# Whole-row transfers around the SSD, early splits of reloaded inputs, and unread products in the conformer's LayerNorm

## The chip, the cores and the metric

The kernel runs on one core of a Trainium2 chip. The metric is the device time of one execution in microseconds (us), as the median of several runs.

## The reference

One inference step of a two-layer decoder trunk, in float32, for a prompt of 512 tokens and a sample group of 8 sequences of 8 tokens. The 576 tokens share all weights; the model has 1024 channels.

```python
# layer 0
xn = rms_norm(x); proj = xn @ w_in_ab           # z | x,B,C | dt | u
ya = mamba2(proj[z, xBC, dt])                   # causal conv of 4, silu, SSD, gate, group norm
yb = s5(proj[u])                                # complex diagonal SSM, gelu, then
yb = y * sigmoid(y @ w_glu + b_glu)             # the gated linear unit (GLU)
x  = x + concat(ya, yb) @ w_out_ab
x  = x + square(relu(rms_norm(x) @ w_ff1)) @ w_ff2
# layer 1
h  = xn @ w_pw1 + b_pw1; h = h[:C] * sigmoid(h[C:])
h  = causal_depthwise_conv(h, 31 taps)
h  = silu(layer_norm(h, ln_w, ln_b))            # mean and variance over 1024 channels
x  = x + h @ w_pw2 + b_pw2
x  = x + square(relu(rms_norm(x) @ w_ff1)) @ w_ff2
y  = rms_norm(x)
```

In the SSD, heads go in 4 groups of 4, and the prompt in 4 chunks of 128 tokens; the 64 sample tokens make a fifth chunk. Each chunk needs exp(cum[i] - cum[j]) for its heads, where cum is the running sum of the log decays.

## The kernel before, in words

**Products.** Activations lie with channels on the 128 partitions and 576 tokens in the free dimension. Each float32 operand is split in two (`split`, L266; `split_scaled`, L257): ScalarE (ACT) writes the high part, VectorE (DVE) the rest. `mm` (L228) multiplies a 128 x 1024 weight tile with eight activation tiles: hi*hi, hi*lo and lo*hi, in two halves of 288 tokens, 48 matmuls on TensorE (PE) for one output tile. `load` (L217) brings the weight tile in on SP's DMA queue and splits it on ACT and DVE (L224, L225), with a priority offset of 3000.

**Order.** The kernel is written once in program order, and a scheduler lays the instructions on each engine's queue by priority and by its own simulated time. `high_priority(n)` moves a block n places up in that order. The queues are fixed then: on the chip each engine, and SP's queue of DMAs, takes its instructions strictly in turn, so one that waits holds all behind it. Tiles of a tag share a ring of buffers: the 17 of tag "B" hold split activations, the 3 of tag "t" hold what comes out of a product or is loaded for one step.

**Layer 0** (`mixer0`, L1061). The products of `w_in` come first: eight for the S5, one for dt, then 24 for the SSD, in four groups of six (B, C, two of x, two of z). Each of the 24 results is copied out of PSUM by `stash` (L759) and stored to DRAM. `side` runs after each product and puts in the other work: first the S5's outputs (`s5_y`, stored to `yg`), then one causal convolution (`a_conv`, L767) and one step of each running SSD group (`a_group`, L879), with an offset of 54 (HPS). Then `reload` (L1154) loads the eight tiles of `yg` and splits them for the eight GLU products; after these it reloads `ybd` for the products with the second half of `w_out`, and last `yad` (the first SSD group's output) for the first half. There the tiles of the other groups are used first, the reloaded ones last.

**The convolution.** `a_conv` loads one stashed tile into `xb`, the prompt and the sample by two DMAs (L773, L774), since each sample sequence gets three tokens of history in front of it: 8 pieces of 11 columns, of which 8 (32 bytes) come from DRAM. DVE scales in place (L776, L777), ACT makes the first tap into `o` (L782), DVE adds three taps (L784) and, after a tanh, closes the silu with one instruction over 600 columns (L787). Two DMAs (L788, L789) store prompt and sample to `xsd`. `xb` and `o` share a ring of three buffers. `a_group` loads its inputs from `xsd` (L889), transposes them on PE (L899), and per chunk loads cum of its 4 heads on all partitions (L943: 4 pieces of 512 bytes each) and exp(cum) (L957); old states come from the input (L924), and the sample's part of the output uses them (L928).

**The conformer** (`conformer`, L1204). The channel means are sums on PE (`mean`, L1301) over the eight convolved tiles; the tile of block 7 is finished last, by DVE (L1389, L1391). Then DVE subtracts the mean (L1259), ACT squares (L1261), DVE adds squares in pairs (L1253), and PE sums each pair over channels by matmuls of one column (`tsum`, L1256). DVE takes the reciprocal root, PE spreads it over the partitions (L323), and DVE and ACT normalise, apply silu and split (L1272 to L1277) in front of the eight products of `w_pw2`.

## Time and profile before

| what | value |
| --- | --- |
| median of 3 runs | 1638.1 us (1636.99 to 1638.96) |
| the profiled execution | 1634.01 us; span 1632.2 us |
| PE busy | 1574.1 us (96% of the span) |
| DVE busy | 1056.4 us (65%) |
| ACT busy | 642.3 us (39%) |
| DMA read, written | 184.1 MB, 34.2 MB |
| mean granted PE clock | 0.975 of full speed |

The profiled execution is 4.1 us under the median of the runs. The span goes from the first to the last instruction; 1.8 us of the execution's time lie around it. A granted clock of 1.0 is 2.4 GHz and 0.5 is 1.2 GHz; it has these two levels, and a number between is a mean over a stretch.

### The profile page before, as it was taken

What the parts mean: (1) busy time and instruction counts of PE and PEld (TensorE: products, weight loads), DVE (VectorE), ACT (ScalarE), POOL (GpSimd) and SP (SyncE); (2) the same over time, 40 slices, a digit from 0 to 9 for tenths busy, and PEclk for the clock granted to TensorE, in tenths of its full rate; (3) what the DMA queues carried; (4) which work ended last, traced back from release to release, by engine and by line L of the source; (5) the groups of instructions that cost most, each with busy time, mean ns of one, the idle gap of its engine ahead of it and who ended that gap; (6) DMA issues with size and microseconds to landing.
All of it is one profiled execution on the core that took longest, in us unless ns stands there. A gap on an engine that the chain in (4) does not pass through costs nothing.

```text
span 1632.2 us, 28709 instructions
## 1 busy us (share of the span) xinstructions
PE 1574.1 (96%) x11765; PEld 1549.3 (95%) x11765; DVE 1056.4 (65%) x1757; ACT 642.3 (39%) x1084; POOL 4.3 (0%) x42
## 2 busy tenths in 40 slices
PE   7999998989899999999999999997899999999997
PEld 6999998889899999999999999996899999999996
DVE  7968986688865547677744457997554444434466
ACT  4243377775643343332222243332443322222243
POOL 0000000000000000000000000000000000000000
PEclk9999999979899999999999999998899999999998
DMA  5644587988863234454322235541122222222233
GB/s 189 184 120 142 158 226 220 298 251 241 241 229 136 78 96 160 156 135 105 101 79 78 91 133 154 167 136 45 42 88 79 78 91 78 79 90 78 91 118 135
DMA packets 185907, 220.18 MB, mean 135 GB/s; under 512 B 92560, under 2 KB 128400, under 8 KB 185776
## 3 DMA queue, kind: packets, MB, share of 16 engines
q1 hardware_dynamic: 182112, 217.03, 44.3%
q8 instruction: 92, 1.51, 0.4%
q10 hardware_dynamic: 3664, 1.32, 0.3%
q14 instruction: 39, 0.32, 0.1%
HBM read 184.10 MB, written 34.20 MB: 134 GB/s over the span
## 4 chain that ended last, share of the span: by engine, by line
PE 84%; DVE 8%; DMA 5%; issue 1%; ACT 1%; SPq 0%; ACTq 0%; DVEq 0%
PE mm L239 76%; PE pc L1326 2%; DVE acc L1389 1%; DVE lo L225 1%; PE yoff L928 1%; DMA by<-s5bc 1%; PE bc L323 1%; DMA eb<-ecd 1%; DMA xsd<-cvo 1%; PE s5s L613 1%; PE kt L572 1%; PE tsum L293 1%; DVE u L589 1%; PE mu L1301 0%; PE yps L952 0%
## 5 line engine op out<-in xcount | busy, mean ns | idle before, releaser
L224 ACT ACTIVATE hi<-raw 128x1024 fp32r<-128x1024 f32 x217 | 229.7, 1059 | 729.4 <-PE mm L239 633.3
L239 PE MATMUL mm<-fxh,hi 128*128 128x288 f32 x1920 | 417.6, 299 | 14.6 <-ACT hi L224 10.4
L225 DVE TENSOR_TENSOR lo<-raw,hi 128x1024 fp32r<-128x1024 f32 x217 | 264.8, 1221 | 248.0 <-ACT hi L224 243.4
L239 PE MATMUL mm<-fxh,lo 128*128 128x288 f32 x1920 | 415.4, 298 | 0.1
L239 PE MATMUL mm<-fxl,hi 128*128 128x288 f32 x1920 | 414.9, 297 | 0.0
L239 PEld LDWEIGHTS mm<-fxh,hi 128*128 128x128 f32 x1920 | 311.5, 190 | 16.3 <-ACT hi L224 11.3
L239 PEld LDWEIGHTS mm<-fxh,lo 128*128 128x128 f32 x1920 | 311.0, 190 | 1.0 <-DVE lo L225 0.7
L239 PEld LDWEIGHTS mm<-fxl,hi 128*128 128x128 f32 x1920 | 311.1, 190 | 0.5 <-issue 0.2
L239 PE MATMUL mm<-gh,lo 128*128 128x288 f32 x1024 | 229.1, 295 | 1.1 <-DVE lo L225 1.1
L239 PE MATMUL mm<-gh,hi 128*128 128x288 f32 x1024 | 229.6, 295 | 0.0
L239 PE MATMUL mm<-gl,hi 128*128 128x288 f32 x1024 | 229.2, 295 | 0.0
L239 PEld LDWEIGHTS mm<-gh,lo 128*128 128x128 f32 x1024 | 167.9, 188 | 1.5 <-DVE lo L225 1.5
L239 PEld LDWEIGHTS mm<-gl,hi 128*128 128x128 f32 x1024 | 168.3, 188 | 0.0
L239 PEld LDWEIGHTS mm<-gh,hi 128*128 128x128 f32 x1024 | 167.9, 188 | 0.0
L363 DVE TENSOR_TENSOR fft<-mm,r2B 128x576 f32<-128x576 f32 x56 | 42.3, 756 | 116.3 <-PE mm L239 116.3
L1389 DVE SCALAR_TENSOR_TENSOR acc<-hb,vec,acc 128x512 f32<-128x512 f32 x110 | 82.2, 747 | 1.5
L357 DVE TENSOR_TENSOR gl<-ffr,gh 128x576 fp32r<-128x576 f32 x64 | 48.4, 757 | 1.9
L356 DVE TENSOR_TENSOR ffr<-ffr 128x576 f32<-128x576 f32 x64 | 48.5, 757 | 1.6
L355 ACT ACTIVATE gh<-ffr 128x576 fp32r<-128x576 f32 x64 | 43.9, 686 | 2.1
L364 DVE TENSOR_TENSOR x<-x,fft 128x576 f32<-128x576 f32 x56 | 42.3, 756 | 1.6
L784 DVE SCALAR_TENSOR_TENSOR cvo<-xb,vh,cvo 128x600 f32<-128x600 f32 x48 | 40.2, 838 | 1.0 <-ACT cvo L782 0.5
L353 ACT ACTIVATE ffr<-mm 128x576 f32<-128x576 f32 x64 | 40.5, 633 | 0.0
(340 smaller groups left out, 1890.0 us busy)
## 6 DMA issues: line engine op xcount, KB each, us to landing
raw<-w_ff SPq DMA_DIRECT2D x136, 512.0 KB, 3.5
raw<-w_in SPq DMA_DIRECT2D x33, 512.0 KB, 3.8
raw<-w_pw SPq DMA_DIRECT2D x24, 512.0 KB, 3.6
dm<-dwm SPq DMA_DIRECT2D x16, 576.0 KB, 5.6
h<-ass SPq DMA_DIRECT2D x16, 512.0 KB, 4.9
raw<-w_out SPq DMA_DIRECT2D x16, 512.0 KB, 3.6
U<-ud SPq DMA_DIRECT2D x16, 288.0 KB, 4.0
prd<-pj SPq DMA_DIRECT2D x16, 288.0 KB, 2.4
```

What stands on the lines that cost most here:

```text
L224: self.last = [nc.sync.dma_start(raw, src), nc.scalar.activation(hi, raw, AF.Copy), eng.tensor_tensor(lo, raw, hi.bitcast(F32), op=ALU.sub ...
L225: eng.tensor_tensor(lo, raw, hi.bitcast(F32), op=ALU.subtract)]
L239: nc.tensor.matmul(ps[:, h, :H], w[:, k], a[:, h * H:(h + 1) * H], start=n == 0, stop=n == 23)
L353: nc.scalar.activation(h2(r), ps, AF.Relu)
L355: nc.scalar.activation(hi, r, AF.Square)
L356: nc.vector.tensor_tensor(r, r, r, op=ALU.mult)
L357: nc.vector.tensor_tensor(lo, r, hi.bitcast(F32), op=ALU.subtract)
L363: nc.vector.tensor_tensor(h2(t), ps, rB, op=ALU.mult)
L364: nc.vector.tensor_tensor(x[m], x[m], t, op=ALU.add)
L784: nc.vector.scalar_tensor_tensor(o[:, 0:600], xb[:, k:k + 600], self.half("acw", 16 * k + m), o[:, 0:600], op0=ALU.mult, op1=ALU.add)
L1326: nc.tensor.matmul(pc[:, g * 128:g * 128 + 128], w[:, j * 128:j * 128 + 128], hq[:, g, j:j + 128], start=j == 0, stop=j == 8)
L1389: nc.vector.scalar_tensor_tensor(ap, hb[:, k:k + NP], w(k), ap, op0=ALU.mult, op1=ALU.add)
```

## The change

- **Whole rows.** `a_conv` loads the 576 columns as they lie in DRAM into `o`, by one DMA; the scaling on DVE reads `o` and writes `xb` with its gaps for the history. The closing DVE instruction becomes two, one for the prompt and one for the sample, which write 576 columns without gaps at the start of `xb`; one DMA stores them. `o` and `xb` now have rings of two each. `cum` is stored in DRAM by chunk, by two DMAs instead of one, so that the 4 heads of a chunk are one piece of 2 KB for each partition. Room for this comes from the odd groups' ring `k1` (4 buffers for 5) and from the dt input, which shares a ring with `yw`.
- **Reloads.** All three calls of `reload` put allocation, DMA and split of each tile at an offset of 1500.
- **Unread products.** `warm(n)` issues n matmuls of 288 columns with operands left by the convolution of block 7, into a PSUM tile that nothing reads, each ordered on PE behind the last matmul before it: 30 in front of the mean of block 7, 20 behind the last mean, 6 behind each of three pair sums, 14 behind the fourth, and 16 behind the spreading of the root: 98 in all.

```diff
--- before.py
+++ after.py
@@ -175,6 +175,7 @@
     GL = 7
     X2 = 8
     HPS = 54
+    HPR = 1500
 
     def X(self, name):
         return self.xp.tile([128, NT], F32, tag="X", name=name)
@@ -320,7 +321,7 @@
         for k in range(c + 1):
             m = 128 if k < c else p
             o = b0[:, k * 128:k * 128 + 128] if k < c else b1[:, 0:p]
-            nc.tensor.matmul(o, cols[:m, k:k + 1].broadcast_to([m, 128]), self.ident[:m, :m], start=True, stop=True)
+            self.pl = nc.tensor.matmul(o, cols[:m, k:k + 1].broadcast_to([m, 128]), self.ident[:m, :m], start=True, stop=True)
         nc.scalar.activation(out[:, 0:128 * c], b0[:, 0:128 * c], AF.Copy)
         nc.scalar.activation(out[:, 128 * c:n], b1[:, 0:p], AF.Copy)
         return out
@@ -767,29 +768,30 @@
     def a_conv(self, m, rB):
 
         nc, q = self.nc, self.q1
-        xb = q.tile([128, 603], F32, tag="cv", name="xb", bufs=3)
+        o = q.tile([128, 603], F32, tag="co", name="cvo", bufs=2)
+        xb = q.tile([128, 603], F32, tag="cv", name="xb", bufs=2)
         s8 = lambda t, k, n: t[:, 515:603].rearrange("p (b j) -> p b j", b=8)[:, :, k:k + n]
+        c8 = lambda t: t[:, NP:NT].rearrange("p (b j) -> p b j", b=8)
         nc.gpsimd.memset(xb[:, 0:3], 0.0)
-        nc.sync.dma_start(xb[:, 3:515], self.prd[m][:, 0:NP])
-        nc.sync.dma_start(s8(xb, 3, 8), self.prd[m][:, NP:].rearrange("p (b j) -> p b j", b=8))
+        nc.sync.dma_start(o[:, 0:NT], self.prd[m])
         nc.scalar.activation(s8(xb, 0, 3), self.aco[:, m, 0:8, :], AF.Copy)
-        nc.vector.tensor_tensor(xb[:, 3:515], xb[:, 3:515], rB[:, 0:NP], op=ALU.mult)
-        nc.vector.tensor_tensor(s8(xb, 3, 8), s8(xb, 3, 8), rB[:, NP:].rearrange("p (b j) -> p b j", b=8), op=ALU.mult)
+        nc.vector.tensor_tensor(xb[:, 3:515], o[:, 0:NP], rB[:, 0:NP], op=ALU.mult)
+        nc.vector.tensor_tensor(s8(xb, 3, 8), c8(o), c8(rB), op=ALU.mult)
         nc.scalar.activation(self.aco[:, m, 8, :], xb[:, 512:515], AF.Copy)
         nc.scalar.activation(self.aco[:, m, 0:8, :], s8(xb, 8, 3), AF.Copy)
 
-        o = q.tile([128, 603], F32, tag="cv", name="cvo", bufs=3)
         nc.scalar.activation(o[:, 0:600], xb[:, 0:600], AF.Identity, scale=self.half("acw", m), bias=self.half("acb", m))
         for k in range(1, 4):
             nc.vector.scalar_tensor_tensor(o[:, 0:600], xb[:, k:k + 600], self.half("acw", 16 * k + m), o[:, 0:600],
                                            op0=ALU.mult, op1=ALU.add)
         nc.scalar.activation(xb[:, 0:600], o[:, 0:600], AF.Tanh)
-        nc.vector.scalar_tensor_tensor(o[:, 0:600], xb[:, 0:600], 1.0, o[:, 0:600], op0=ALU.add, op1=ALU.mult)
-        nc.sync.dma_start(self.xsd[m][:, 0:NP], o[:, 0:NP])
-        nc.sync.dma_start(self.xsd[m][:, NP:].rearrange("p (b j) -> p b j", b=8), s8(o, 0, 8))
+        d = xb[:, 0:NT]
+        nc.vector.scalar_tensor_tensor(d[:, 0:NP], xb[:, 0:NP], 1.0, o[:, 0:NP], op0=ALU.add, op1=ALU.mult)
+        nc.vector.scalar_tensor_tensor(c8(d), s8(xb, 0, 8), 1.0, s8(o, 0, 8), op0=ALU.add, op1=ALU.mult)
+        nc.sync.dma_start(self.xsd[m], d)
 
     def a_dt_in(self, ps, rB):
-        df = self.qs.tile([128, NT], F32, tag="dtf", name="dtf", bufs=1)
+        df = self.qs.tile([128, NT], F32, tag="yw", name="dtf", bufs=2)
         with self.hp(self.HPE):
             self.nc.vector.tensor_tensor(h2(df)[:32], ps[:32], h2(rB)[:32], op=ALU.mult)
         return df
@@ -870,7 +872,9 @@
         ch = self.qs.tile([128, NT], F32, tag="u3", name="ch", bufs=self.U3)
         nc.scalar.activation(ch[:16, 0:NP], c0[:16], AF.Copy)
         nc.scalar.activation(ch[:16, NP:], c1[:16, 0:64], AF.Copy)
-        nc.sync.dma_start(self.cumd, ch[:16])
+        cd = lambda o, *ap: bass.AP(tensor=self.cumd.tensor, offset=self.cumd.offset + o, ap=[list(k) for k in ap])
+        nc.sync.dma_start(cd(0, (128, 16), (2048, 4), (1, 128)), ch[:16, 0:NP].rearrange("h (c t) -> h c t", c=4))
+        nc.sync.dma_start(cd(16 * NP, (64, 16), (1, 64)), ch[:16, NP:])
         ec = self.u3("ec", NT)
         nc.scalar.activation(ec[:16, 0:NT], ch[:16], AF.Exp)
         nc.sync.dma_start(self.ecd, ec[:16, 0:NT])
@@ -880,7 +884,7 @@
         nc = self.nc
         u = str(g % 2)
         k2 = lambda name, *sh: q.tile([128, *sh], F32, tag="sg" + u, name=name, bufs=3)
-        k1 = lambda name, *sh: q.tile([128, *sh], F32, tag="k1" + u, name=name, bufs=5)
+        k1 = lambda name, *sh: q.tile([128, *sh], F32, tag="k1" + u, name=name, bufs=5 - g % 2)
         hg = slice(4 * g, 4 * g + 4)
         hp = lambda t: t.rearrange("p (h d) -> p h d", h=4)
 
@@ -940,8 +944,11 @@
                 nc.scalar.activation(xw[:T, e * 64:(e + 1) * 64], xt[:T, c, e * 64:(e + 1) * 64], AF.Copy,
                                      scale=self.dw[:T, c, 4 * g + e:4 * g + e + 1])
             sg = k2("sg", 4, 128)
-            nc.sync.dma_start(sg[:, :, :T], bass.AP(tensor=self.cumd.tensor, offset=self.cumd.offset + 4 * g * NT + t0,
-                                                    ap=[[0, 128], [NT, 4], [1, T]]))
+            src = lambda *ap: bass.AP(tensor=self.cumd.tensor, offset=self.cumd.offset + 16 * t0 + 4 * g * T, ap=[[0, 128], *ap])
+            if c < 4:
+                nc.sync.dma_start(sg.rearrange("p h t -> p (h t)"), src([1, 4 * T]))
+            else:
+                nc.sync.dma_start(sg[:, :, :T], src([T, 4], [1, T]))
             for e in range(4):
 
                 nc.scalar.activation(sg[:T, e, :T], sg[:T, e, :T], AF.Relu, scale=-1.0, bias=self.cum[:T, c, 4 * g + e:4 * g + e + 1])
@@ -1154,9 +1161,10 @@
             def reload(d, f):
                 out = []
                 for k in range(len(d)):
-                    t = self.t("rl", "t")
-                    nc.sync.dma_start(t, d[k])
-                    out.append(f(k, t))
+                    with self.hp(self.HPR):
+                        t = self.t("rl", "t")
+                        nc.sync.dma_start(t, d[k])
+                        out.append(f(k, t))
                 return out
 
             act = reload(self.yg, lambda k, t: self.split(t, "y", self.B))
@@ -1241,7 +1249,10 @@
             self.dwconv(q, 7, hbs[7], acc[7])
             for m in self.ORD:
                 if m not in done:
+                    if len(done) == 6:
+                        self.warm(30)
                     self.mean(mu, acc, m, done)
+            self.warm(20)
             nmu = q.tile([128, NT], F32, tag="nmu", name="nmu", bufs=1)
             for h in range(2):
                 nc.scalar.activation(nmu[:, h * H:h * H + H], mu[h][:, 0:H], AF.Copy)
@@ -1253,7 +1264,7 @@
                 dve.append(nc.vector.tensor_tensor(sq[n], sq[n], sq[n + 1], op=ALU.add))
                 for c in (0, 4, 1, 2, 3):
                     m = min(128, NT - c * 128)
-                    nc.tensor.matmul(ts[:m, c:c + 1], sq[n][:, c * 128:c * 128 + m], self.ones[:, 0:1], start=n + c == 0, stop=(n, c) == (6, 3))
+                    self.pl = nc.tensor.matmul(ts[:m, c:c + 1], sq[n][:, c * 128:c * 128 + m], self.ones[:, 0:1], start=n + c == 0, stop=(n, c) == (6, 3))
 
             for n, k in enumerate(self.ORD):
                 dve.append(nc.vector.tensor_tensor(acc[k], acc[k], nmu, op=ALU.add))
@@ -1261,11 +1272,14 @@
                 nc.scalar.activation(sq[n], acc[k], AF.Square)
                 if n in (2, 4, 6):
                     pair(n - 2)
+                    self.warm(6)
             pair(6)
+            self.warm(14)
             self.chain(dve)
             r = self.tp.tile([128, 5], F32, tag="r5", name="r5")
             self.rstd_tok((ts, 4, 64), 1024, r)
             rB = self.bcast_tok(r, "rBl")
+            self.warm(16)
             act, dve, sca = [], [], []
             for k in range(9):
                 if k < 8:
@@ -1295,10 +1309,18 @@
         self.dd, self.de = tiles("dd", [128, 4, 136]), tiles("de", [128, 4, 128])
         self.dm = {}
 
+    def warm(self, n):
+
+        w, a = self.wh
+        ps = self.pm.tile([128, 2, 512], F32, tag="mm", name="warm")
+        with self.tc.issue_after(self.pl.ins):
+            for k in range(n):
+                self.nc.tensor.matmul(ps[:, k % 2, :H], w[:, k % 4], a[:, :H], start=True, stop=True)
+
     def mean(self, mu, acc, m, done):
 
         for h in range(2):
-            self.nc.tensor.matmul(mu[h][:, 0:H], self.neg, acc[m][:, h * H:h * H + H], start=not done, stop=len(done) == 7)
+            self.pl = self.nc.tensor.matmul(mu[h][:, 0:H], self.neg, acc[m][:, h * H:h * H + H], start=not done, stop=len(done) == 7)
         done.append(m)
 
     def dwconv_mat(self, q, m, g):
@@ -1382,6 +1404,8 @@
                     i = m * 31 + k + j
                     nc.scalar.activation(dh[:, j], self.ident, AF.Copy, scale=self.wdh.bitcast(F32)[:, i:i + 1])
                     nc.scalar.activation(dl[:, j], self.ident, AF.Copy, scale=self.wdl[:, i:i + 1])
+                if n == 4:
+                    self.wh = dh, hh
                 for j in range(n):
                     for i, (dd, h) in enumerate(((dh, hh), (dh, hl), (dl, hh))):
                         nc.tensor.matmul(pc, dd[:, j], h[:, k + j:k + j + NP], start=k + j == k0 and i == 0, stop=k + j == 30 and i == 2)
```

## Rows read from the trace of the kernel before

**Rows 1.** The page's chain of work that ended last, shares by engine.

```profile
PE 84%; DVE 8%; DMA 5%; issue 1%; ACT 1%; SPq 0%; ACTq 0%; DVEq 0%
```

**Rows 2.** Windows: the SSD's stretch; busy PE, PEld, DVE, ACT, POOL; clock, DMA share, GB/s.

```profile
215.00:500.00 285.00, 266.16 (x1974) 253.86 (x1973) 221.06 (x416) 179.56 (x431) 1.62 (x15) 0.92 0.82 241
```

**Rows 3.** Waits of PE, 215 to 500 us: total us, times, longest us.

```profile
PE tr L899 <- DMA xs<-xsd: 6.5, 2, 3.4
PE yoff L928 <- DMA h<-ass: 2.3, 1, 2.3
PE mm L239 <- ACT ybh L261: 2.0, 1, 2.0
PE mm L239 <- DVE yl L272: 1.5, 1, 1.5
...
PE mm L239 <- ACT yh L271: 0.9, 1, 0.9
```

**Rows 4.** Timeline of PE, 1104 to 1166 us: start, us, and idle time before.

```profile
1126.45 3.71 PE L1301 MATMUL mu<-acc,neg 128*128 128x288 f32 x8 [4.69 <-DVE acc L1391]
...
1133.63 8.84 PE L1256 MATMUL tsum<-ones,sq 128*128 128x1 f32 x40 [3.47 <-DVE sq L1253]
...
1144.95 2.66 PE L323 MATMUL bc<-cst,r 128*128 128x128 f32 x10 [2.48 <-DVE rv L302]
...
1150.33 1.33 PE L239 MATMUL mm<-fxh,hi 128*128 128x288 f32 x4 [2.72 <-ACT fxh L1275]
```

**Rows 5.** Windows in the LayerNorm; columns as in rows 2.

```profile
1123.00:1126.00 3.00, 0.00 (x0) 0.00 (x0) 2.79 (x5) 0.00 (x0) 0.00 (x0) 1.00 0.00 0
...
1135.00:1138.00 3.00, 2.93 (x15) 2.80 (x15) 2.92 (x5) 1.98 (x3) 0.00 (x0) 0.50 0.01 3
```

**Rows 6.** Chain in order of time: pieces at full clock, then first products of `w_pw2`.

```profile
561.50 0.99 PE tsum L293 x10
...
570.66 1.25 PE bc L323 x10
...
708.62 273.46 PE mm L239 x2051
...
1077.23 0.97 PE mu L1301 x4
...
1150.33 14.31 PE mm L239 x92
```

**Rows 7.** Timeline of DVE, 1104 to 1166 us: the last pair of squares.

```profile
1139.41 0.76 DVE L1253 TENSOR_TENSOR sq<-sq 128x576 f32<-128x576 f32 x1 [0.81 <-ACT sq L1261]
```

**Rows 8.** Timeline of DVE, 312 to 346 us: the first split of `yg`.

```profile
328.29 1.53 DVE L990 SCALAR_TENSOR_TENSOR ya<-xf,vec,ya 128x576 f32<-128x576 f32 x2
329.75 0.74 DVE L272 TENSOR_TENSOR yl<-rl,yh 128x576 fp32r<-128x576 f32 x1
```

**Rows 9.** Timeline of SP's DMA queue, 305 to 335 us.

```profile
324.32 0.32 SPq L765 DMA_DIRECT2D zsd<-pj  x1
...
330.23 0.94 SPq L1158 DMA_DIRECT2D rl<-yg  x2
```

**Rows 10.** Timeline of SP's DMA queue, 400 to 412 us.

```profile
401.03 2.09 SPq L789 DMA_DIRECT2D xsd<-cvo  x1
406.36 0.32 SPq L773 DMA_DIRECT2D xb<-prd  x1
...
407.26 0.52 SPq L924 DMA_DIRECT2D h<-ass  x1
```

**Rows 11.** Waits of SP's queue, 215 to 500 us.

```profile
SPq L773 <- DMA xsd<-cvo: 11.2, 6, 3.1
```

**Rows 12.** DMA issues of the whole span: count, KB each, median us to landing.

```profile
xb<-prd SPq DMA_DIRECT2D x16, 256.0 KB, 3.7
...
xb<-prd SPq DMA_DIRECT2D x16, 32.0 KB, 3.7
```

**Rows 13.** Groups by line, 215 to 500 us: a DVE instruction on the sample's columns.

```profile
L777 DVE TENSOR_TENSOR xb<-xb,rB 128x64 f32<-128x64 f32 x16 | 3.5, 220 | 0.0
```

**Rows 14.** Timeline of DVE, 462 to 512 us: the last split of `ya`.

```profile
500.33 1.55 DVE L262 SCALAR_TENSOR_TENSOR yal<-ya,vec,yah 128x576 fp32r<-128x576 f32 x2 [0.18 <-ACT yah L261]
```

**Rows 15.** Timeline of PE, 495 to 512 us: the first product with `ya`.

```profile
503.66 0.42 PE L239 MATMUL mm<-yah,hi 128*128 128x288 f32 x2
```

## The prediction

> **What bounds the kernel now.** I read the chain of work that ended last first: TensorE (PE) holds 84% of it, DVE 8% and DMA 5% [rows 1]. PE's matmuls stay as they are, so the change can only give back what PE loses: time in which it waits, and time in which it runs at 1.2 GHz. The windows show two places. In the SSD's stretch of 285 us PE is busy 266.2 us, so 18.8 us are idle, and its mean clock is 0.92 [rows 2]; with levels 0.5 and 1.0 that is 0.16 x 285 = 45.6 us at half speed. PE's waits there say who ends the idle time [rows 3]: transposes that wait for a load from `xsd` (6.5 us) and matmuls that wait for old states (2.3), both by DMA, and 4.4 us in which the products wait for splits of a reloaded input (2.0 + 1.5 + 0.9). The second place is the LayerNorm: PE's timeline has four waits, 4.69, 3.47, 2.48 and 2.72 us [rows 4]. The windows there show the clock at 1.00 during the first wait and at 0.50 while PE is busy 2.93 of 3.00 us with one-column sums [rows 5]. So a wait costs its own time and then slow matmuls behind it.
>
> **Price of a wait in the SSD's stretch.** The eight matmuls of the last means took 3.71 us at low clock [rows 4], twice 0.97 at full [rows 6]: 1.9 times as long, so a slow microsecond of work loses 0.47 us. If half of the idle time lies inside the slow time, (45.6 - 9.4) x 0.47 = 17 us are lost beside 18.8 us of waits: each microsecond of wait costs about 1.9 us, an estimate from these rows.
>
> **Unread products.** A product at full clock takes 273.46 / 2051 = 0.133 us [rows 6]. Thirty take 4.0 us and fit into the wait of 4.69 us. What they hold up is the mean queued behind them on PE, which DVE releases later anyway; were DVE faster, they would cost up to 4.0 us. With the clock up, the eight matmuls of the means take 1.94 us for 3.71: -1.8 us. The chain of DVE and ACT behind them starts that much earlier.
>
> Next, the four pair sums. They took 8.84 us for 40 matmuls at low clock [rows 4], 4 x 0.99 at full [rows 6]. Before, they ended at 1142.47 us, 2.3 us after DVE's last pair at 1139.41 + 0.76 [rows 7]. At full clock they would end at 1138.4 + 1.0: -3.1 us with the -1.8 in it. Spreading the root would take 1.25 us [rows 6] instead of some 2.4 (1.9 times that): -1.1. The first 92 products of `w_pw2` took 14.31 us [rows 6], 2.0 more than 92 x 0.133. All that is -6.2 us, one end. The other: the clock falls among the pairs. Then each pair costs 2.2 us of sums and 6 x 0.133 x 1.9 = 1.5 of fillers, 3.7 us against DVE's 2.2 from pair to pair ((1140.17 - 1133.63) / 3), and the sums end about 13.3 us after their start at 1131.9, 2.7 us later than before; 30 fillers at low clock (7.6 us) overrun the waits of 2.48 and 2.72 by 2.3. With -2.0 for the products that end is +3.0.
>
> I take -2.5. The means (-1.8) and the first products (-2.0) have long bursts of fillers in front of them; for the pairs I charge +1.3, since the nearest row shows one-column sums that keep PE busy and the clock low [rows 5], and six fillers are only 0.8 us of each 2.2. The Trainium skill, "TensorE: Matmul & The Clock Gate", section "Why this matters for your kernels", asks only for no long idle gaps between bursts of matmuls, and by it every wait here is bridged and the sum is -6.2. The trace of before agrees as to gaps; in rows 5, PE had hardly a gap and stayed slow.
>
> **Reloads in front.** At the first GLU product PE waits for the split of `yg`: DVE does two steps of the SSD (1.53 us) first, then `yl` [rows 8]. The priority removes this kind of delay; nothing is computed twice, so ACT and DVE pay nothing more. The pool is the 4.4 us of rows 3, 8.4 us with the clock. Not all of it can go: the tag "t" has three buffers, and the third reload follows the store of the last z product, issued at 324.32, with its own load at 330.23 [rows 9]. That chain of store, load and split stays, only with less in front. I take half, -4.2. On SP, eighteen loads move past SSD loads; the latter are late by 18 issues in all, and that hides behind the products as long as the SSD's end has slack (below).
>
> **Whole rows.** 32 DMAs go (two of four per convolution), one comes with `cum`. The landing does not shorten by that: the piece of 256 KB and the sample's 32 KB both land after 3.7 us in the median [rows 12], side by side. What changes is the buffers. SP's queue stands 11.2 us in six waits for a store of `xsd`, because the load's buffer is the one that the store reads [rows 11]; with the new rings the load waits only for DVE. One such stand is plain: SP finishes issuing a store at 403.12 and issues the next load at 406.36, and the load of old states behind it only at 407.26 [rows 10]. PE waits 2.3 us for these states; issued 3.2 us earlier they cause no wait: 2.3 x 1.9 = -4.4 us. After that, ACT or DVE is late next, since the write into `xb` still waits for the store. For the 6.5 us behind `xsd` I take nothing: it is one store and one load in a row as before. If the queues were so much emptier that it went too, the part would be worth 8.8 x 1.9 = -16.7, the low end. The added DVE instruction on the sample's columns costs about 0.22 us [rows 13], 16 times 3.5 us; DVE is idle 64 us of the stretch [rows 2] and hides it; uncovered it is +3.5, the high end. The 2 KB pieces of `cum`, the smaller ring `k1` and the shared ring of dt have no row; I bound them by the waits of rows 3, none of which names them, and take 0.
>
> **Sum.** -2.5 - 4.2 - 4.4 = -11.1 us. Against the profiled execution (1634.0 us: the span of 1632.2 and 1.8 around it) that is 1622.9; the median of the runs stands 4.1 us higher, so I predict 1627.0 us.
>
> **Rivals.** A measurement of this kernel can tell about 0.2% (3.3 us) from no change.
>
> *The clock stays up* through the whole LayerNorm: -6.2 instead of -2.5, 1623.3 us. For it: every wait is bridged. Against it: the slow clock of a busy PE [rows 5]. 12%. This is also what the rule of the Trainium skill named above would give.
>
> *The SSD's waits mostly go* too: -14 from the two other parts, -6.2 here, 1617.9 us. For it: all these waits stem from in-order queues. Against it: the SSD's end. Its last split ends at 500.33 + 1.55 = 501.88 [rows 14]; PE starts the products with `ya` at 503.66 [rows 15] and reaches this tile after 4 x 6 products, at 506.9. So there are 5.0 us of slack, and a larger gain needs a faster SSD as well. 13%.
>
> *Given back, or not done*: the reloads cannot start earlier, as their buffers come from the last products, and the queues, laid anew, stall elsewhere. Then only the LayerNorm's -2.5 stays: 1635.6 us. 20%.
>
> *Slower*: ACT stands in order in front of the third split, because its load hangs on a store that is later on the chip than the scheduler believes. The stand is up to 5.9 us between the two issues [rows 9] plus 3.7 of landing (nearest row, [rows 12]): 9.6 us, at two reloads 19.2. The SSD's work behind it is late; above 5.0 us of it PE waits at the SSD's end, up to 14.2 us. Half of that, less 2.5, is +4.6: 1642.7 us. Against it: SSD work that ACT has done before the split is not late. 15%.
>
> **How the numbers follow.** The forecast gets 40%. Faster by over 0.2%: 40 + 12 + 13, and a third of the fourth case's 20 (7): 72%. Within 0.2%: the rest of that case (13) and 1 of the last: 14%. Slower: 14%. The range goes from 1617, where the SSD's waits mostly go, to 1639, which takes in the given-back case; it leaves out most of the slower case and the far side of the large gain, some 18%.
>
> **What would show it.** In the LayerNorm: the means at about 1.9 us for eight matmuls, the clock at 1.00 there and at the first products, perhaps 0.50 among the pairs. PE's waits by split of a reloaded input: half of 4.4 us or less. SP's waits for a store of `xsd` at its loads gone, and no wait of PE for old states. PE's idle time between 215 and 500 us down from 18.8 to about 14. I am wrong if PE waits at the SSD's end for `ya`, if ACT's waits for reloads exceed 5 us, or if the one-column sums end later than before relative to the means.

## The result, and the profile after

| what | value |
| --- | --- |
| median of 4 runs | 1617.7 us (1613.1 to 1623.3) |
| the kernel before, beside it | 1638.5 us (1637.0 to 1639.4) |
| ratio, 95% interval | 0.9876 [0.9842, 0.9909], so -20.3 us (-25.9 to -14.9) |
| the profiled execution | 1619.07 us; span 1617.3 us |
| PE, DVE, ACT busy | 1575.4 (97%), 1057.3 (65%), 641.1 us (40%) |
| DMA read, written | 184.1 MB, 34.2 MB, as before |
| mean granted PE clock | 0.986 |

The changed kernel is faster, by nearly twice the forecast of 11.1 us, and inside the range by 0.7 us at its low end (1617). The two profiled executions differ by 14.9 us, since that of before lies 4.1 us under its median and that of after 1.4 us over its own; what follows reads these two.

**Where the time came from.** PE reaches the first product with `ya` at 487.82 us for 503.66 [rows 15], 15.8 us earlier; the last eight matmuls of the means at 1111.55 for 1126.45 [rows 4], 14.9 earlier; the span ends 14.9 earlier. All of it comes from the SSD's stretch and nothing from the LayerNorm.

The windows of the kernel after, the SSD's stretch (the columns and bounds of [rows 2]):

```profile
215.00:500.00 285.00, 273.82 (x2099) 261.71 (x2098) 229.69 (x440) 183.79 (x438) 1.61 (x15) 0.96 0.76 250
```

PE is idle 285 - 273.8 = 11.2 us for 18.8, the clock is 0.96 for 0.92, and the DMA engines move more (250 GB/s for 241) in less of their time (0.76 for 0.82). PE's waits in that stretch (for [rows 3]), then one of SP's queue and one of ACT:

```profile
PE tr L903 <- DMA xs<-xsd: 4.5, 2, 2.3
PE mm L240 <- ACT yh L272: 3.8, 2, 3.5
PE yps L959 <- DVE xd L942: 1.6, 1, 1.6
```

```profile
SPq L893 <- DMA xsd<-xb: 3.6, 5, 1.1
```

```profile
ACT xb L777 <- DMA xsd<-xb: 15.8, 10, 4.2
```

The wait for old states (2.3 us) is gone, and those for the splits of `ybd`; that for `yh` has grown from 0.9 to 3.8. SP's 11.2 us at the convolution's load [rows 11] are gone. ACT, which writes into `xb`, waits more for the store than before. SP's wait for the store at the load of an SSD input, from which the prediction took nothing, has shrunk as well. In the trace of before these two were:

```profile
ACT xb L775 <- DMA xsd<-cvo: 11.0, 7, 4.7
```

```profile
SPq L889 <- DMA xsd<-cvo: 9.2, 6, 4.7
```

Six more traces (e4, e5, e6, e9, e10 and e13 of the experiments below) have the changed kernel's order on PE and on SP's queue up to the first product with `ya`. In all of them the wait for old states is gone and SP's wait at L893 is 3.5 to 4.1 us; PE's waits for splits of `yg` are 2.2 to 4.1 us, and its idle time in this window is 11.4 to 14.9 us. So a single wait, read in one trace, is good to some 2 us.

The LayerNorm, timeline of PE of the kernel after (for [rows 4]):

```profile
1106.55 4.33 PE L1318 MATMUL warm<-hh,dh 128*128 128x288 f32 x30
1111.55 2.21 PE L1323 MATMUL mu<-acc,neg 128*128 128x288 f32 x8 [0.67 <-DVE acc L1415]
1113.38 3.01 PE L1318 MATMUL warm<-hh,dh 128*128 128x288 f32 x20
1117.23 1.40 PE L1267 MATMUL tsum<-ones,sq 128*128 128x1 f32 x10 [0.84 <-DVE sq L1264]
1118.50 1.79 PE L1318 MATMUL warm<-hh,dh 128*128 128x288 f32 x6
1120.09 2.09 PE L1267 MATMUL tsum<-ones,sq 128*128 128x1 f32 x10
...
1127.16 2.09 PE L1267 MATMUL tsum<-ones,sq 128*128 128x1 f32 x10
...
1132.37 1.42 PE L324 MATMUL bc<-cst,r 128*128 128x128 f32 x10
...
1136.64 0.80 PE L240 MATMUL mm<-fxh,hi 128*128 128x288 f32 x4 [0.54 <-ACT fxh L1289]
```

The means run at full clock (2.21 us for 3.71). The first pair sum begins so (1.40), and from the second on each takes 2.09 and the six fillers behind it 1.79: the clock fell among the pairs. The windows of the kernel after give the place:

```profile
1117.23:1118.38 1.15, 1.15 (x10) 1.12 (x10) 1.15 (x2) 0.50 (x1) 0.00 (x0) 1.00 0.00 0
1118.40:1120.09 1.69, 1.69 (x9) 1.69 (x9) 1.61 (x4) 0.87 (x3) 0.00 (x0) 0.50 0.00 0
...
1127.16:1132.03 4.87, 4.87 (x23) 4.84 (x23) 1.96 (x14) 0.00 (x0) 0.00 (x0) 0.50 0.00 0
1132.05:1136.00 3.95, 3.95 (x30) 3.62 (x28) 1.43 (x2) 1.68 (x4) 0.00 (x0) 1.00 0.02 4
```

It is 0.50 for 13.65 us, until the 14 fillers behind the last sum have nearly run.

### The profile page after: what moved, and what is told of

Its sections match the earlier page's. It is cut to its first block, busy times and chain, and to the rows that moved or that the text cites. A ratio compares the mean times of both kernels' runs of the same rounds, so it can differ in the third digit from the quotient of the medians.

```text
span 1617.3 us, 28913 instructions
## 1 busy us (share of the span) xinstructions
PE 1575.4 (97%) x11863; PEld 1552.1 (96%) x11863; DVE 1057.3 (65%) x1773; ACT 641.1 (40%) x1084; POOL 4.3 (0%) x42
## 3 DMA queue, kind: packets, MB, share of 16 engines
q10 hardware_dynamic: 3664, 1.32, 0.3%
## 4 chain that ended last, share of the span: by engine, by line
PE 83%; DVE 8%; DMA 6%; ACT 2%; issue 1%; SPq 1%; ACTq 0%; DVEq 0%
PE mm L240 73%; DVE acc L1413 2%; PE pc L1348 2%; DVE lo L226 1%; DMA xs<-xsd 1%; DVE cvo L785 1%; DMA rl<-yg 1%; PE bc L324 1%; DMA yg<-y 1%; PE yoff L932 1%; PE s5s L614 1%; DMA ud<-u 1%; PE kt L573 1%; PE s5y L718 1%; PE s5y L719 1%
## 5 line engine op out<-in xcount | busy, mean ns | idle before, releaser
L240 PE MATMUL mm<-fxh,hi 128*128 128x288 f32 x1920 | 415.4, 298 | 12.6 <-ACT hi L225 10.5
L240 PEld LDWEIGHTS mm<-fxh,hi 128*128 128x128 f32 x1920 | 310.2, 189 | 14.2 <-ACT hi L225 11.5
```

Of the source, the lines that this page charges most:

```text
L240: nc.tensor.matmul(ps[:, h, :H], w[:, k], a[:, h * H:(h + 1) * H], start=n == 0, stop=n == 23)
```

## The experiments

"Off" is the ratio's distance from 1, with its interval, times the median of before in the same set of runs (1638.5 us for the changed kernel, 1640.1 for e1 to e4, 1639.8 for e5 to e8, 1638.6 for e9 to e13). "LN" is the time in the profiled execution from the start of the last eight mean matmuls to the start of the 96th product of `w_pw2`; "low" is the longest time for which the clock then stood at 0.50. Kernels without fillers have an LN of 37.8 to 39.6 us; their LayerNorm is the same, so these 1.8 us are the spread from trace to trace.

| run | median us | ratio | off, us | LN, us | low, us |
| --- | --- | --- | --- | --- | --- |
| after | 1617.7 | 0.9876 [0.9842, 0.9909] | -20.3 | 38.27 | 13.65 |
| e1_rows_only | 1628.0 | 0.9928 [0.9901, 0.9955] | -11.8 | 39.32 | 30.72 |
| e2_reload_only | 1636.3 | 0.9973 [0.9955, 0.9991] | -4.4 | 39.61 | 30.72 |
| e3_fill_only | 1638.5 | 0.9986 [0.9967, 1.0004] | -2.3 | 38.46 | 13.65 |
| e4_no_fill | 1620.7 | 0.9875 [0.9849, 0.9902] | -20.5 | 38.35 | 20.48 |
| e7_conv_rows | 1627.5 | 0.9916 [0.9897, 0.9936] | -13.8 | 38.12 | 20.48 |
| e8_rings_only | 1630.7 | 0.9946 [0.9928, 0.9964] | -8.9 | 39.25 | 30.72 |
| e12_rows_yg | 1620.6 | 0.9887 [0.9868, 0.9906] | -18.5 | 37.83 | 20.48 |
| e5_no_pair_fill | 1620.7 | 0.9880 [0.9859, 0.9900] | -19.7 | 36.21 | 10.24 |
| e9_bridge_26_6 | 1617.2 | 0.9875 [0.9855, 0.9895] | -20.5 | 36.93 | 10.24 |
| e10_bridge_20_8 | 1620.5 | 0.9895 [0.9874, 0.9915] | -17.2 | 40.52 | 17.07 |
| e6_denser_pair_fill | 1616.6 | 0.9853 [0.9831, 0.9875] | -24.1 | 33.75 | none |
| e13_all_bridged | 1615.9 | 0.9865 [0.9845, 0.9885] | -22.1 | 33.76 | none |

### One part at a time

**Whole rows alone**: the changed kernel without the early reloads and without fillers.

```diff
-                    with self.hp(self.HPR):
+                    with self.hp(0):
...
-                        self.warm(30)
...
-            self.warm(20)
...
-                    self.warm(6)
...
-            self.warm(14)
...
-            self.warm(16)
```

> Only the whole-row part: convolution rings and transfers, and cum stored by chunk. Theory (the SSD's queues give the gain, and each of the two SSD parts its share): SP no longer waits for a store of xsd at the convolution's loads, PE's wait for old states goes, 6 to 10 us faster than before (1629 to 1633). Rival (the order of the reloads is what counts): within 3 us of before, and PE's waits for splits of reloaded inputs stay at about 4 us. Rival (the two parts need each other): within 3 us.

Measured: -11.8 us (-16.2 to -7.4). The windows (columns of [rows 2]) and PE's waits of this run:

```profile
215.00:500.00 285.00, 271.77 (x2074) 258.72 (x2073) 227.50 (x439) 183.23 (x437) 1.60 (x15) 0.95 0.75 249
```

```profile
PE yps L959 <- ACT hst L985: 4.5, 2, 4.0
PE tr L903 <- DMA xs<-xsd: 2.0, 2, 1.4
```

The wait behind `xsd` is down from 6.5 to 2.0 us, and there is none for old states. A new one of 4.5 us, for ACT's state of an SSD step, takes a part back. PE idles 13.2 us, 5.6 less, and is at the first product with `ya` at 492.77, 10.9 earlier.

**Early reloads alone**: the kernel before with `high_priority` of 1500 around the reload.

```diff
-                    t = self.t("rl", "t")
-                    nc.sync.dma_start(t, d[k])
-                    out.append(f(k, t))
+                    with self.hp(self.HPR):
+                        t = self.t("rl", "t")
+                        nc.sync.dma_start(t, d[k])
+                        out.append(f(k, t))
```

> Only the reloads at an offset of 1500. Theory: the first GLU product starts some 4 us earlier, PE's waits for reloaded splits fall by half, 4 to 8 us faster than before (1631 to 1635). Rival (the rows and rings are what counts): within 3 us of before, the time saved at the reloads is lost at the SSD's DMAs. Rival (the two parts need each other): within 3 us.

Measured: -4.4 us (-7.4 to -1.5). The first GLU product did not start some 4 us earlier, as expected, but 3.6 us later (331.30 us for 327.69; 2.2 of it stood already in front of the SSD's stretch), and PE's idle time between 215 and 500 us fell only from 18.8 to 17.4 us; the clock there rose from 0.92 to 0.95. What stops the gain is the SSD's end. Its last splits on DVE (for [rows 14]) and PE's one wait there:

```profile
508.56 1.55 DVE L263 SCALAR_TENSOR_TENSOR yal<-ya,vec,yah 128x576 fp32r<-128x576 f32 x2 [0.17 <-ACT yah L262]
```

```profile
508.58 0.79 PE L240 MATMUL mm<-yah,hi 128*128 128x288 f32 x4 [2.10 <-ACT yah L262]
```

PE was at the first product with `ya` 6.2 us earlier than before (497.48), but the SSD was done at 510.11 for 501.88, 8.2 us later: together 14.4 us, against the slack of 5.0 that the prediction read there. In this kernel's queue 48 products and some small matmuls stand in front of the late tile, for 24 products before, and PE still waits 2.1 us.

**Both, without fillers**:

```diff
-                        self.warm(30)
...
-            self.warm(20)
...
-                    self.warm(6)
...
-            self.warm(14)
...
-            self.warm(16)
```

> The whole change without the unread products. Theory: 1618 to 1623, all but some 2 us of the gain, and 16 us of it in front of the first product with ya. Rival (the fillers carry a third or more): 1625 or more. If the two SSD parts add up, this run lies as far below before as the whole-row run and the reload run together; if they need each other, it lies further.

Measured: -20.5 us (-24.8 to -16.1), the whole gain of the change. Behind the whole rows the reloads are worth 20.5 - 11.8 = 8.7 us, for 4.4 alone. That they are worth more there is not shown by the times: the two parts alone add up to 16.2 us, just inside the interval of both. The traces give a reason why it could be so: whole rows end the SSD earlier (last split at 486.15 + 1.54 = 487.69 in the changed kernel), and PE does not wait there.

**Fillers alone**: the 98 products in the kernel before.

```diff
+                    if len(done) == 6:
+                        self.warm(30)
...
+            self.warm(20)
...
+                    self.warm(6)
...
+            self.warm(14)
...
+            self.warm(16)
```

> Only the unread products; the queues of DVE, ACT and SP stand as before, and PE's has 98 matmuls more. Theory: the fillers bring the eight matmuls of the last means to 1.9 us and the first products of w_pw2 to full clock, but the pair sums run slow between them: from the first of these means to the last of the first 96 products 0 to 2.5 us less than before, and 0 to 3 us in the median. Rival (the medians of the changed kernel lie further below than its profile, so the fillers give more in other runs): 5 us or more.

Measured: -2.3 us (-5.4 to +0.7), not told from nothing. Its profiled execution took 1640.8 us and was 7.5 us late at the last means already, so its whole time says little; its LN of 38.46 us beside 38.41 before says that these fillers gained nothing there. Between the changed kernel and the one without fillers there is nothing either (0.9876 and 0.9875).

### Whole rows: buffers or pieces

**The convolution's rows without the change of `cum`** (its loads too are as before; no early reloads, no fillers):

```diff
-        cd = lambda o, *ap: bass.AP(tensor=self.cumd.tensor, offset=self.cumd.offset + o, ap=[list(k) for k in ap])
-        nc.sync.dma_start(cd(0, (128, 16), (2048, 4), (1, 128)), ch[:16, 0:NP].rearrange("h (c t) -> h c t", c=4))
-        nc.sync.dma_start(cd(16 * NP, (64, 16), (1, 64)), ch[:16, NP:])
+        nc.sync.dma_start(self.cumd, ch[:16])
...
```

> The kernel before with the convolution's whole rows and its two rings alone (with the smaller k1 ring and the shared dt buffer that make the room); cum stored as before, reloads as before, no unread products. The same with all of the whole-row part, cum by chunk too, took 12.0 us off. Theory: the rings give it, since the convolution's load no longer waits for the store; 8 to 12 us faster than before (some 1628 to 1632), and no wait of PE for old states. Rival: the 2 KB pieces of cum give a good part (512-byte pieces four times as many compete with the other transfers): then less than 7 us faster, above 1633.

Measured: -13.8 us (-16.9 to -10.5). It is no slower than with the 2 KB pieces of `cum` (-11.8), so these gave nothing that shows.

**The same with the transfers of before**: rings of two for `o` and `xb`, but each load and store in two DMAs with the 32-byte pieces, and one closing instruction on DVE as before.

```diff
-        nc.sync.dma_start(o[:, 0:NT], self.prd[m])
+        nc.sync.dma_start(o[:, 3:515], self.prd[m][:, 0:NP])
+        nc.sync.dma_start(s8(o, 3, 8), self.prd[m][:, NP:].rearrange("p (b j) -> p b j", b=8))
...
-        nc.sync.dma_start(self.xsd[m], d)
+        nc.sync.dma_start(self.xsd[m][:, 0:NP], xb[:, 0:NP])
+        nc.sync.dma_start(self.xsd[m][:, NP:].rearrange("p (b j) -> p b j", b=8), s8(xb, 0, 8))
```

> As the run with the convolution's whole rows, but with two DMAs for each load and each store and the 32-byte pieces of the sample as before: the two rings alone. Theory: the pieces don't matter, the buffers do (32 KB in 1024 pieces landed after 3.7 us as 256 KB did): within 3 us of the whole-row run and 7 to 12 us faster than before. Rival: the pieces matter, because 65 thousand packets fewer leave the DMA engines room: then within 3 us of before, and the whole-row run is 8 us or more below it.

Measured: -8.9 us (-11.8 to -5.9). Neither reading holds alone: the rings give about two thirds. Its six runs (1629.5 to 1633.4) all lie above the six with whole rows (1623.4 to 1629.2), so the pieces count too, 3.3 us by the medians. The windows of the two, whole rows first:

```profile
215.00:500.00 285.00, 270.06 (x2050) 257.37 (x2048) 228.08 (x441) 183.07 (x437) 1.61 (x15) 0.95 0.76 246
```

```profile
215.00:500.00 285.00, 265.26 (x2000) 252.76 (x1999) 222.51 (x417) 179.14 (x433) 1.61 (x15) 0.94 0.83 242
```

With the pieces the DMA engines are busy 0.83 of the time for 242 GB/s, without them 0.76 for 246. The pages show the pieces themselves, whole rows first; the difference is 33 thousand packets, and not the 65 thousand of the expectation:

```profile
DMA packets 152627, 220.17 MB, mean 135 GB/s; under 512 B 59281, under 2 KB 95121, under 8 KB 152497
```

```profile
DMA packets 185908, 220.18 MB, mean 135 GB/s; under 512 B 92561, under 2 KB 128401, under 8 KB 185777
```

Between these two the landing is shorter too: median us from issue to landing of the store and of the SSD's input, whole rows first:

```profile
xsd<-xb SPq DMA_DIRECT2D x16, 288.0 KB, 3.7
xs<-xsd SPq DMA_DIRECT2D x16, 288.0 KB, 5.5
```

```profile
xsd<-xb SPq DMA_DIRECT2D x16, 256.0 KB, 4.8
```

```profile
xs<-xsd SPq DMA_DIRECT2D x16, 288.0 KB, 6.5
```

The load of cum goes from 6.8 to 5.4 us and the convolution's load from 4.3 to 3.9. This is one trace each, and it does not hold against the other kernels: in the changed kernel the convolution's load and store land after 4.6 and 5.2 us, for 3.7 [rows 12] and 4.3 before. How the lower load of the DMA engines becomes PE's time was not shown. The profiled execution with the rings alone is no help: it is the second longest of its six, PE idles 19.7 us in it, and it waits 5.5 us for old states, although the convolution's load no longer waits for the store. SP's wait for the store at the load of an SSD input is 4.1 us in it, for 9.2 before.

### Which reload

**Whole rows with the reload of `yg` alone early**, no fillers:

```diff
-                    with self.hp(self.HPR):
+                    with self.hp(self.HPR if d is self.yg else 0):
```

> The whole rows with the reload of yg alone at the offset of 1500 (ybd and yad as before), no unread products. Whole rows alone were 11.8 us under before, with all three reloads 20.5. Theory: the reload of yg adds little, since PE still waits for its splits with the offset (3.8 us in the changed kernel, 3.1 without the unread products, 2.4 before: the chain of store, load and split stays); the two later reloads and a shorter SSD's end give the rest. Then this is within 4 us of whole rows alone (11 to 16 us faster than before). Rival: the early splits of yg give most of what the reloads add, because DVE and ACT then do the SSD's work later in one piece: 17 us or more faster than before, and PE's waits for yh and yl below 1 us in all.

Measured: -18.5 us (-21.6 to -15.4). The time is the rival's (17 or more), though the interval ends just inside the theory's 11 to 16: `yg` alone adds 6.7 us to whole rows, most of the 8.7, and the offsets of `ybd` and `yad` add nothing that shows. But the rival's reason is not what the waits show:

```profile
PE tr L903 <- DMA xs<-xsd: 4.6, 3, 1.8
PE yps L959 <- DVE xd L942: 2.5, 2, 2.1
PE mm L240 <- DVE yl L273: 1.0, 1, 1.0
```

Waits for splits of `yg` are 1.0 + 0.5 us here, 1.0 + 0.3 with whole rows alone. What went is the 4.5 us behind ACT's state of an SSD step; with all three reloads early that wait is nothing in two traces and up to 2.5 us in the five others. The early splits change the order of the SSD's work on the queues; I don't know which step of it counts, so the cause of this part stays open.

### The LayerNorm's fillers

**Without the six at the pairs:**

```diff
-                    self.warm(6)
```

> The changed kernel without the six unread products behind each of three pair sums (the 30, 20, 14 and 16 stay). Theory: in the changed kernel the clock falls among the pairs all the same (0.5 from 1118.4 to 1132.0 us), so each pair costs 2.09 us of sums and 1.79 of fillers, 3.9 us against DVE's 2.2 from pair to pair, and the sums take 12.0 us where the kernel without any fillers takes 8.84. Without the six the sums are again paced by DVE: the last of them ends 2 to 4 us earlier relative to the means, and the time is 1 to 3 us below the changed kernel (some 1615 to 1617 beside 1617.7). Rival: the six keep the clock up for a part of the sums or bring it back sooner for the spreading of the root and the first products; then the time is the same or up to 3 us above the changed kernel.

Measured: LN 36.21 us, 2.1 less than with them, and the last sum ends 14.53 us after the means' start for 17.70, both as the theory had it. The median (1620.7) lies above the changed kernel's and not 1 to 3 us below: a difference of this size isn't resolved by the runs, whose intervals are 7 to 11 us wide.

**Eight for six, and 26 for 20 behind the means:**

```diff
-            self.warm(20)
+            self.warm(26)
...
-                    self.warm(6)
+                    self.warm(8)
```

> The changed kernel with eight unread products for six behind each of three pair sums, and 26 for 20 behind the last mean. Theory: the clock falls among the pairs because PE still has idle gaps there at full clock: 0.99 us of sums and 6 x 0.133 = 0.80 of fillers are 1.8 us of each 2.2; with eight they are 2.05, and the clock stays at 1.00 through the pairs. Then the sums end 3 to 4 us earlier than in the changed kernel, the spreading of the root takes 1.25 us, and the time is 3 to 5 us below the changed kernel. Rival: the one-column sums by themselves let the clock fall, whatever fills the gaps; then each pair costs 2.1 + 8 x 0.27 = 4.2 us or more, and the time is 1 to 2 us above the changed kernel, about 4 above the one without the six.

Measured: LN 33.75 us, 4.5 less than the changed kernel, as the theory had it, and 4.7 less than before; the ratio is the lowest of all. The timeline of PE:

```profile
1116.68 3.80 PE L1318 MATMUL warm<-hh,dh 128*128 128x288 f32 x26
1120.54 1.35 PE L1267 MATMUL tsum<-ones,sq 128*128 128x1 f32 x10
1121.75 1.30 PE L1318 MATMUL warm<-hh,dh 128*128 128x288 f32 x8
1122.88 1.24 PE L1267 MATMUL tsum<-ones,sq 128*128 128x1 f32 x10
...
1127.38 1.24 PE L1267 MATMUL tsum<-ones,sq 128*128 128x1 f32 x10
```

All four sums run at full clock.

**The two numbers apart, 26 and six, then 20 and eight:**

```diff
-            self.warm(20)
+            self.warm(26)
```

> The changed kernel with 26 unread products for 20 behind the last mean; the six at the pairs stay. With 20 PE stood 0.84 us before the first pair sum, and the clock fell 2.0 us after that stand; with 26 and eight at each pair there was no stand and the clock held. Theory: the stand behind the means is what lets the clock fall; bridged, the clock is 1.00 through the four pair sums with six products too, the sums end 13 to 14 us after the start of the last eight mean matmuls (17.7 in the changed kernel, 13.8 with 26 and eight), and the 96th product of w_pw2 comes 33.5 to 34.5 us after it (38.3 and 33.8). Rival: the short stands that six leave at each pair (about 0.3 us of each 2.2) let it fall all the same, only later: then the sums end 15 us or more after the means' start and the 96th product comes 36 us or more after it.

```diff
-                    self.warm(6)
+                    self.warm(8)
```

> The changed kernel with eight unread products for six at each pair; the 20 behind the last mean stay, so the stand of 0.84 us before the first pair sum stays. Theory (the stand behind the means decides): the clock falls in the first or second pair as in the changed kernel, each pair then costs 2.1 + 8 x 0.3 = 4.5 us, the sums end 18 to 20 us after the start of the last eight mean matmuls, and the 96th product of w_pw2 comes 38.5 to 40.5 us after it. Rival (the stands at the pairs decide): the clock holds, and the 96th product comes at 33.5 to 35 us.

Measured: 26 and six 36.93 us, the rival's figure; 20 and eight 40.52 us, the theory's. So both count, by one trace of each. With 20, PE stands 0.83 us before the first sum and the clock falls in the first fillers behind it; eight fillers at the pairs then only cost more (4.01 us a pair). With 26 the stand is gone, and with six the clock falls all the same, in the second pair. The windows of the run with 26 and six:

```profile
1120.78:1122.96 2.18, 2.18 (x16) 1.99 (x17) 2.10 (x4) 1.36 (x2) 0.00 (x0) 1.00 0.00 0
1122.96:1124.28 1.32, 1.32 (x12) 1.29 (x12) 1.28 (x2) 0.67 (x2) 0.00 (x0) 1.00 0.00 0
1124.30:1127.60 3.30, 3.30 (x17) 3.27 (x17) 2.19 (x3) 1.34 (x2) 0.00 (x0) 0.50 0.00 0
```

PE is busy in all of it, so the rival's reason (short stands at each pair) finds no support: the clock falls without a stand that the trace shows. The ends of matmuls are modelled there, so a stand hidden in a matmul's time would not show.

**Every wait filled**: 28, 26, 8, 18 and 20.

```diff
-                        self.warm(30)
+                        self.warm(28)
...
-            self.warm(14)
+            self.warm(18)
...
-            self.warm(16)
+            self.warm(20)
```

> The changed kernel with 28 for 30 in front of the last mean, 26 for 20 behind it, eight for six at the pairs, 18 for 14 behind the fourth sum and 20 for 16 behind the spreading: the best guess for all waits of the LayerNorm. Theory: the clock stays at 1.00 from the means to the first products; against 26 and eight alone two stands of 0.53 and 0.54 us are filled, which gains nothing at full clock (the products wait for DVE and ACT anyway), so the 96th product comes 33.5 to 34 us after the start of the last eight mean matmuls, and the time is 3 to 5 us under the changed kernel as it stands, some 1613 to 1616. Rival: the longer fillers overrun the work they cover and hold up the spreading and the first products by 0.5 us each: 34.5 us or more.

Measured: LN 33.76 us, the same as with 26 and eight. It and that run have the lowest medians (1615.9 and 1616.6). Both beat the kernel before; that they beat the changed kernel is shown by the LN alone (33.75 and 33.76 us for 38.27, one profiled execution each), and not by the medians, whose intervals overlap. The mean clock over the whole of an execution, which is known for every run, fits with exceptions: it is 0.990 to 0.992 in all four runs of 26 and eight, and 0.985 to 0.987 in three of four of the changed kernel, but 0.992 in its fourth, its shortest (1613.1 us), and 0.986 in the longest run with every wait filled (1619.5 us). Whether the clock falls among the pairs may thus differ between executions of one kernel; a trace shows one of them. A kernel with `yg` alone early and these fillers was not tried, nor a third buffer for `xb`.

## Why the prediction was right, and where it was off

**The price of a wait held in four runs and failed in three.** Idle time and clock between 215 and 500 us gave 1.9 us for each microsecond of wait. Measured, by what PE's first product with `ya` came earlier, over what its idle time fell: 15.8 / 7.7 = 2.1 in the changed kernel, 10.9 / 5.6 = 1.9 with whole rows alone, 18.1 / 8.3 = 2.2 with `yg` early, 6.6 / 3.9 = 1.7 with the convolution's rows. But the change without fillers has 15.1 / 5.8 = 2.6, the early reloads alone 6.2 / 1.4 = 4.3, and the rings alone came 1.9 us earlier with 0.9 us more idle time. The time at half speed does not go in step with the waits: it was 44.4 us before, 20.5 in the changed kernel, and 13.7, 30.7 and 34.1 in these three, by the clock's records in the traces. So the price is a mean over this kernel's waits and no rule for the next one.

**Whole rows: the term was mis-sized, -4.4 for -11.8.** The step that failed is "For the 6.5 us behind `xsd` I take nothing: it is one store and one load in a row as before". In a row they stand, but not at the old distance. The order of SP's queue, before and after, where PE had its longest such wait before (3.41 us at 264.79):

```profile
256.12 0.32 SPq L788 DMA_DIRECT2D xsd<-cvo  x1
256.49 0.43 SPq L789 DMA_DIRECT2D xsd<-cvo  x1
261.67 0.32 SPq L889 DMA_DIRECT2D xs<-xsd  x1
262.09 0.38 SPq L773 DMA_DIRECT2D xb<-prd  x1
```

```profile
255.97 0.32 SPq L791 DMA_DIRECT2D xsd<-xb  x1
256.34 0.43 SPq L776 DMA_DIRECT2D cvo<-prd  x1
...
257.76 0.42 SPq L791 DMA_DIRECT2D xsd<-xb  x1
258.87 0.32 SPq L893 DMA_DIRECT2D xs<-xsd  x1
```

Before, SP stood 4.75 us from the end of the store's issue (256.92) to the load. After, the next convolution's load goes out right behind the store, a second store follows, and the first load of an input leaves at 258.87. In both traces that load leaves when the store has landed, 5.1 us after its issue before and 2.8 after. Why the store lands sooner here is not shown; the pieces are not needed for it, as the store in this place, the third of `xsd`, landed after 2.1 and 2.5 us with its pieces in the run with the rings alone. The prediction had the mechanism, a queue that a store holds up, and a row for it [rows 11], beside which the 9.2 us at L889 stand in the same view; it asked which wait of PE the convolution's load ends directly, and not which stores and loads stand behind it. Its low end of -16.7 had the price of all of it. The step on old states was right in the changed kernel (2.3 us gone), but not a rule: in the run with the convolution's rows alone 2.5 us of that wait are there, and 5.5 with the rings alone.

**"A larger gain needs a faster SSD as well" was right, and read as evidence against.** The SSD's end does bound the reloads when they stand alone. But whole rows make the SSD faster: its last split ended 14.2 us earlier (487.69 for 501.88), nearly as much as PE's first product with `ya`. I held the two parts apart and added them. Measured, both together gave 4.3 us more than the sum of the two alone, a difference that the intervals do not resolve.

**Reloads: the size held alone (-4.2 for -4.4), by luck.** The forecast was half of 4.4 us of waits, with their price in clock. Alone, the waits for `ybd` went (2.0 us) and those for `yg` fell from 2.4 to 2.0 us, but others came, PE's idle time fell by 1.4 us in all, and most of what PE was early by was clock. In the changed kernel the waits for `yg` grew to 3.8 us, so the sign "half of 4.4 us or less" failed there; the chain of store, load and split stays, as predicted. What the early reload of `yg` gives behind whole rows (6.7 us) does not come from these waits.

**LayerNorm: -2.5 for nothing.** The means: -1.5 for -1.8, since the eight take 2.21 us at full clock and not twice 0.97; of the 3.71 before, the first 0.55 were at full clock. The first products: -1.4 for -2.0 (96 of them in 13.18 us for 14.53). The pairs: from the means' end to the first product 22.88 us for 20.17 before, +2.7 where I charged +1.3. The mechanism was named, as the other end: the clock falls among the pairs, and each costs 3.7 us. It was 3.53. By that end the sums end 2.7 us later than before, counted from the means' start, and the last fillers overrun by 2.3 more; measured, they end 17.70 us after it for 16.02, 1.7 later, and nothing overran. That the sums end later was one of the prediction's own signs of being wrong, and it came: for the LayerNorm the forecast was wrong, and the charge half of what was needed. With 26 fillers and eight the clock held as in the end of -6.2, and -4.7 came: -1.5 at the means, -1.8 from there to the first product, -1.4 at the first products.

The Trainium skill, "TensorE: Matmul & The Clock Gate", section "Why this matters for your kernels", wants no long idle gaps between bursts of matmuls. Here the gap of 0.83 us with 20 mattered (LN 40.52 us, for 33.75 with 26, eight at the pairs in both), but the run with 26 and six fell to 0.50 with PE busy in the whole stretch before; the measurement goes beyond that rule.

**The rivals.** The time is that of the rival in which the SSD's waits mostly go (1617.9 us), given 13%. Its SSD term was -14, where the change without fillers measured -20.5; its -6.2 for the LayerNorm did not come. That the two errors cancel is luck, and so is it that the time lies within the range, whose low bound is this rival's. The rival *slower* is refuted: PE waits for nothing at the SSD's end. My mark for it was badly set: ACT's waits for reloads do exceed 5 us (16.1 in all, the longest 6.0), but those of before came to 14.2 by 510 us, with a longest of 5.8.

## What to carry to other kernels

Where an in-order queue stands behind a store, price all that is queued behind it, not only the wait that it ends directly: a load that needs a buffer from a store in flight should have another buffer. A speed-up that stops at a deadline can be worth more together with one that moves the deadline (8.7 us for 4.4 here, within noise), so test the pair and not the parts alone. Fillers that do not keep the clock up are slow themselves and cost more than they bring: here six at each pair gave an LN of 38.27 us, none 36.21, and eight, with the wait in front filled too, 33.75. A price per wait taken from one trace is no rule: count idle time and time at half speed apart.

## What the runs showed of the hardware

- In the run with 26 and six the granted clock fell at 1124.29 us with PE busy 1.32 of 1.32 and 2.18 of 2.18 us before: one-column sums with six products of 288 columns between them. With eight between them, in the run with 26 and eight, it stayed at 1.00 through all four sums.
- Once down, fillers of six or eight products between the sums did not bring it back; in all five runs where it fell there it rose within 2 us of the end of the 14 products in a row (0.5 us before it to 1.8 after), after 10.24 to 17.07 us. Without any filler it stayed low for 20.48 to 30.72 us.
- The 32 KB in 32-byte pieces landed no later than the 256 KB beside them (3.7 us both [rows 12]), and yet dropping the pieces took the busy share of the DMA engines from 0.83 to 0.76 (242 and 246 GB/s), the landing of the SSD's input loads from 6.5 to 5.5 us, and 3.3 us off the time.
